# The down product of experts with 65 to 128 tokens: one slice in plain fp32, three with split operands

## The chip, the core and the metric

The kernel runs on one core of a Trainium2 chip. The metric is the device time of one execution, in microseconds (us). It is written in Bass and Tile: every engine (PE is the matrix engine, DVE the vector engine, ACT the scalar engine, POOL the GpSimd engine, SP the engine that issues most DMAs) has its own stream of instructions, and semaphores order them.

## The reference, cut to what matters

Two layers of a diffusion backbone over 1024 latent and 256 context tokens, model width 1024. Each layer ends in a mixture of 32 experts, of which every token takes two. In layer 1 1280 tokens go through it, in layer 2 1024. For the tokens `xb` of expert `e`:

```
return (jax.nn.silu(xb @ wg[e]) * (xb @ wu[e])) @ wd[e]
```

`wg` and `wu` are 1024 x 512, `wd` is 512 x 1024, all fp32: 6.3 MB for each expert. The row is then scaled by its gate and added to the token.

## The kernel before, in words

The function `moe` holds the whole of a layer's experts. They are taken in an order by size that the router writes into a table on the chip (behind the first FIX = 2), so how many tokens each step of the unrolled loop has is known only at run time: `n` is that number in blocks of 64, and `tc.If` picks one of the written variants. `n` = 1 runs `half` (64 tokens), `n` = 2 (65 to 128 tokens, the case that the change touches) runs `full`, and `n` over 2 runs `large`, which lies in the code between the test of `n` (L2345) and the other two variants (L2349).

Weights come through a ring of 14 buffers of 1 MB (the names er, es, raw, ox), six units for an expert: units 0 to 3 hold two slices each of gate and up, units 4 and 5 two slices each of `wd`. SP issues their loads in `e_loads` (L2046, L2048), four units ahead of the activation and two behind the evacuation, each when the buffer that it fills is free. So the ring runs some two experts ahead.

A product in plain fp32 is one `matmul`. A product "with split operands" is `mm3` (L173): each operand is a high part, which ACT makes by rounding to fp32r (`split`, L170), and a low part, which DVE makes as the difference (L171); then three fp32r products are added up (high x high L175, low x high L176, high x low L177). `full` (L2132) forms gate and up so: eight slices `k`, each of two halves `o`, 48 matmuls. The split weights lie in four pairs of buffers WS[0] to WS[3] (wh, wl). Slices 0 to 2 are split ahead by `prep` (L2097) together with the tokens (xh, xl); slice `k` + 3 is split while slice `k` is multiplied, and slices 6 and 7 are multiplied half by half.

Behind `full` each engine goes on in this order:

- DVE copies two columns of places (L2364); ACT forms the silu of both halves (L2163) and DVE multiplies (L2164) into sg.
- PE transposes the next expert's tokens xg (L2082) and sg (L2170) in turns; ACT copies the transposed sg to g (L2171), and ACT and DVE copy the next expert's tokens to xT (L2087, L2088).
- `down` (L2177) multiplies g by `wd` in plain fp32: four slices for each of two halves, 8 matmuls of 128 x 512 (L2181) into py[0] and py[1]. ACT and DVE have no work in it.
- If the next expert has `n` > 1, `prep` splits its slices 0 to 2 and its tokens (L2393): on ACT wh, xh, wh, xh, wh, on DVE wl, xl, wl, xl, wl.
- `evac` copies py[0] on ACT (L2186) and py[1] on DVE (L2187) to my. SP issues the next loads, POOL scatters my to memory (L2195).
- Then the next expert's test of `n` follows, and in its `full` ACT and DVE begin with the split of slice 3.

So ACT and DVE meet `prep`, then the evacuation, then slice 3, strictly in this order.

Of the kernel before, what the change touches and what calls it, by code (L numbers as in the profile page):

```python
# [10 lines left out]
F32R = mybir.dt.float32r  # L11
# [34 lines left out]

FIN = {'G': 'AAAPPPPP', 'C': 'PPPDPDDD', 'E': 'AAAAAAAA', 'N': 'SPSPSPSS'}
P1 = {'C': 'DPDPPPPDPP', 'E': 'AADAADDDAA', 'N': 'SSDSPSPDSS', 'W': 'DPDDDDDP', 'W2': 'DPPDDDDP', 'H': 'DDPDDDPDDP', 'V': 'AADDADDAADDAAADDADAA', 'U': 'AADAD'}
# [11 lines left out]
class Plan:  # L60
# [7 lines left out]
    def add(self, eng, length, f, deps=(), rank=(0.0, ""), at=0.0, take=None, give=(), after=None):  # L68

        e = [eng] if isinstance(eng, str) else list(eng)
        n = [length] if isinstance(eng, str) else list(length)
        fs = [f] if isinstance(eng, str) else list(f)
        k = len(self.ops)
        self.ops.append((list(zip(e, n, fs)), sorted({d for d in deps if d is not None}), rank, at, take, after))
        for g in give:
            self.givers.setdefault(g, []).append(k)
        return k
# [65 lines left out]
class Kernel:  # L145
# [555 lines left out]
    def plan1(self, order, sp, below, raws, Wh, Wl, PS, load, where, pb):  # L701
# [126 lines left out]
        def block_ops(n):  # L828
# [66 lines left out]
            def close(j):  # L895
                ps = PS[b, j]
                ip, ic = where((b - CT // 2 if last else b) * 256)
                if j == 0:
                    if P1["U"][n] == "D":
                        v.tensor_copy(self.U[:, :, ip:ip + 256], ps)  # L900
                    else:
                        act.activation(self.U[:, :, ip:ip + 256], ps, AF.Copy)
                    return
                v.tensor_tensor(self.A[:, j - 1, ic:ic + 256], ps[:, 1, :], sgs[j], op=OP.mult)
            sgs = {}

            def sigm(j):
                sgs[j] = below.tile([128, 256], F32, name="sg", bufs=2)
                act.activation(sgs[j], PS[b, j][:, 0, :], AF.Sigmoid)
# [23 lines left out]
            for j in range(3):  # L933
# [3 lines left out]
                else:  # L937
                    x = add(ACT, 0.26, lambda j=j: sigm(j), [ends[j]] + ([SG[m - 3]] if m > 3 else []))
                    SG[m] = CL[m] = add(DVE, 0.34, lambda j=j: close(j), [x, ma])

        SG, W2L = {}, []
        tile_ops(0)
# [1108 lines left out]
    def moe(self):  # L2051
        tc, nc, l = self.tc, self.nc, self.l
        nt = self.nt
        T = nt * 128
        with ExitStack() as ctx:
            sp = ctx.enter_context(self.pool(f"ms{l}", bufs=1))
# [5 lines left out]
            py = [pp.tile([128, 512], F32, name=f"mpy{o}", bufs=1) for o in range(2)]  # L2062
            scat = []
            self.ring += [wp.tile([128, 2048], F32, name=f"es{i}") for i in range(NU - NU0)]
            WS = [(wp.tile([128, 1024], F32R, name=f"wh{i}"), wp.tile([128, 1024], F32R, name=f"wl{i}")) for i in range(NS)]
            G = [sp.tile([128, 4, 128], F32, name=f"g{i}") for i in range(2)]
            SG = [sp.tile([128, 256], F32, name=f"sg{i}") for i in range(2)]
            iv = sp.tile([128, 3], I32, name="iv")
            XT = [sp.tile([128, KD, 128], F32, name=f"xT{i}") for i in range(2)]
# [20 lines left out]
            def xt(x, n):  # L2090
                xt_copy(xt_pe(x), n)
# [33 lines left out]
            def prod(ps, i, k, ns=NS, os=range(2)):  # L2125
                h, lo = [w.rearrange("p (s n) -> p s n", s=2) for w in WS[k % ns]]
                for o in os:
                    c = slice(o * 256, o * 256 + 256)
                    self.mm3(ps[o], XS[i][0][:, k, :], XS[i][1][:, k, :], h[:, :, c], lo[:, :, c],
                             k == 0, k == KD - 1)  # L2130

            def full(ps, e, x=None):  # L2132

                for k in range(KD - 2):
                    if k + AHEAD < KD:
                        ws(e, k + AHEAD)
                    prod(ps, 0, k)
                for o in range(2):
                    for k in range(KD - 2, KD):
                        prod(ps, 0, k, NS, (o,))  # L2140
                    if x is not None and o == 0:
                        xt(x, e)

            def double(ps, p2, e, m):

# [15 lines left out]
            def act(ps, o):  # L2161
                sg = SG[o]
                nc.scalar.activation(sg, ps[o][:, 0:256], AF.Silu)  # L2163
# [13 lines left out]
            def down(g, e, hf, os=range(2)):  # L2177
                for k, o in [(k, o) for k in range(4) for o in os] if hf else [(k, o) for o in os for k in range(4)]:
                        c = slice(o * 512, o * 512 + 512)
                        z = k // 2 * 64  # L2180
                        nc.tensor.matmul(py[o][64 * o:64 * o + 64, :] if hf else py[o],  # L2181
                                         g[:, k % 2, z:z + 64] if hf else g[:, k, :],
                                         self.unit(e, 4 + k // 2)[:, k % 2, c], start=(k == 0), stop=(k == 3))
# [151 lines left out]
            for e in range(NE):  # L2335
                n = N.pop(e)
                nxt = e + 1 if e + 1 < NE else None
                if e + 3 < NE:
                    load_n(e + 3)
                if e + 2 < NE:  # L2340
                    gather(xg[e % 2], first(e + 2, 0, "a"))
                ps, p2, y, y2, g, g2 = GU[e % 2], GU[1 - e % 2], Y[e % 2], Y[1 - e % 2], G[e % 2], G[1 - e % 2]
                if e < NE // 2:

                    with tc.If(n > 2, preferred_fallthrough_block=True) as c:  # L2345
                        large(e, n, ps, p2, y2, g2)
                        nc.tensor.addr_align(256, offset=0, max_nops=0)
                    with c.Else():
                        with tc.If(n > 1, preferred_fallthrough_block=True) as c2:  # L2349
                            full(ps, e)  # L2350
                        with c2.Else():
                            half(ps, e)
                else:
                    with tc.If(n < 2) as c:
                        half(ps, e)
                    with c.Else():
                        with tc.If(n > 2) as c2:
                            large(e, n, ps, p2, y2, g2)
                        with c2.Else():
                            full(ps, e)  # L2360
                self.e_loads(e * 6 + 4 + NU)
                pl = sp.tile([128, 2], I32, name="pl", bufs=4)
                for o, z in enumerate((self.idx_v, self.idx_w)):
                    nc.vector.tensor_copy(pl[:, o:o + 1], z[:, 0, at(e)])  # L2364
                if e + 3 < NE:
                    over(e + 3)
                s0, s1 = act(ps, 0), act(ps, 1)
                if nxt:
                    x = xt_pe(xg[nxt % 2], (0,))
                ht(ps, s0, g, 0)  # L2370
                if nxt:
                    x += xt_pe(xg[nxt % 2], (1,))
                ht(ps, s1, g, 1)
                if nxt:
                    xt_copy(x, nxt)
                if e < NE // 2:
                    with tc.If(n > 2, preferred_fallthrough_block=True) as c:
                        large_down(e, n, p2, y2, g, g2, pl)
                    with c.Else():
                        with tc.If(n > 1, preferred_fallthrough_block=True) as c2:  # L2380
                            down(g, e, False)
                        with c2.Else():
                            down(g, e, True)
                else:
                    with tc.If(n < 2) as c:
                        down(g, e, True)
                    with c.Else():
                        with tc.If(n > 2) as c2:
                            large_down(e, n, p2, y2, g, g2, pl)
                        with c2.Else():  # L2390
                            down(g, e, False)
                if nxt:
                    with tc.If(N[nxt] > 1):  # L2393
                        prep(nxt)
                evac(y)
                self.e_loads(e * 6 + 6 + NU)
                scatter(y, [pl[:, o:o + 1] for o in range(2)])
                if e >= NE - 3:
                    self.marks.append(nc.gpsimd.memset(self.spacer, 0.0))
                if e == 2:  # L2400
                    self.route_gates()

    def final(self):
# [3 lines left out]
        with ExitStack() as ctx:  # L2407
# [14 lines left out]
            def tile_ops(i):  # L2422
# [7 lines left out]
                if i > 4:  # L2430
                    XL[i] = add(DMA, 1.45, lambda: self.comb_xload(t), [Y.get(3)])
                if FIN["G"][i] == "A":
                    x = add(ACT, 1.04, lambda: self.comb0a(i, t), [y])
# [115 lines left out]
```

## Time and profile before

| what | us |
|---|---|
| median of 3 runs | 3205.91 |
| lowest and highest run | 3199.2, 3206.66 |
| the profiled execution, its own time | 3205.89 |
| its span, first to last instruction | 3204.1 |
| PE busy | 2653.9 |
| DVE busy | 1507.2 |
| ACT busy | 1187.7 |
| POOL busy | 1064.8 |

The profiled execution took what the median took (0.02 us apart), and 1.8 us of it lie outside its span. Its mean granted TensorE clock is 0.916 of full speed. Busy shares are averages over very different stages: layer 1's experts run from about 876 to 1640 us of the span, layer 2's from about 2390 to 3138.

### The profile page before, as it was taken

The page shows a single profiled execution, that of the slowest core. Times are in us where ns is not written, and L with a number is a line of the kernel's source. Part 1 is how long each engine was busy: PE and PEld are TensorE (multiplying, and loading weights), DVE is VectorE, ACT ScalarE, POOL GpSimd, SP SyncE. Part 2 cuts the span into 40 slices and gives each one's busy share as a digit, 9 for nine tenths or more (in the row PEclk, how much of TensorE's full clock was granted, in tenths as well). Part 3 has the DMA queues.
Part 4 walks back from the last instruction along what each step waited for, and adds up shares of the span by engine and source line. Part 5 has one row for each costly group of instructions (what it writes and reads, how often), then busy time and mean ns, then how long its engine had stood idle before and what let it go on. Part 6 is the DMA issues. An engine that isn't in the chain of part 4 may idle for free. (4 is left out here: it accounts for less than half of the span.)

```text
span 3204.1 us, 43663 instructions
## 1 busy us (share of the span) xinstructions
PE 2653.9 (83%) x13122; PEld 1670.8 (52%) x13122; DVE 1507.2 (47%) x2981; ACT 1187.7 (37%) x2260; POOL 1064.8 (33%) x919
## 2 busy tenths in 40 slices
PE   6988899998489888987748989999848888887873
PEld 3766556576356445543317765566634455632321
DVE  3355556477644345521149555556852335511115
ACT  3223766632043334511135337665202335511112
POOL 1023999223311121111236349941331111112214
PEclk8988999999699999999978999999969999999987
DMA  7542000042665558899985530002274457799995
GB/s 268 216 139 81 1 1 1 1 157 79 236 245 189 198 181 307 311 351 361 349 315 186 185 136 1 1 1 99 86 260 167 158 196 267 294 363 369 354 357 238
DMA packets 280646, 617.02 MB, mean 193 GB/s; under 512 B 63376, under 2 KB 77072, under 8 KB 271504
## 3 DMA queue, kind: packets, MB, share of 16 engines
q1 hardware_dynamic: 253872, 566.43, 49.0%
q0 software_dynamic: 24544, 37.91, 3.4%
q8 instruction: 281, 4.60, 0.6%
q10 hardware_dynamic: 1536, 4.69, 0.4%
q14 instruction: 413, 3.38, 0.3%
HBM read 577.09 MB, written 73.81 MB: 203 GB/s over the span
## 5 line engine op out<-in xcount | busy, mean ns | idle before, releaser
L2195 POOL DMA_INDIRECT y_d<-my,pl x150 | 166.1, 1107 | 451.2 <-ACT wh L170 194.5
L1330 DVE TENSOR_REDUCE mx<-S 128x1 f32<-128x1024 f32 (+1 forms) x272 | 215.3, 799 | 210.7 <-PE S L1325 210.4
L2181 PE MATMUL mpy<-er,g 128*64 128x512 f32 (+1 forms) x656 | 239.7, 665 | 6.9 <-issue 6.7
L2194 POOL MEMSET spacer<- 128x1 f32 x152 | 17.5, 115 | 665.9 <-DMA y_d<-my,pl 520.5
L175 PE MATMUL gu<-wh,xh 128*128 128x512 f32 x432 | 183.2, 424 | 47.1 <-issue 12.6
L2082 PE MATMUL mtp<-ident,xg 128*128 128x128 f32 x600 | 107.2, 314 | 138.9 <-issue 85.6
L2163 ACT ACTIVATE sg<-gu 128x256 f32<-128x256 f32 x152 | 50.3, 383 | 461.3 <-PE gu L2115 313.9
L1342 ACT ACTIVATE P<-S,nb 128x256 f32<-128x256 f32 (+1 forms) x272 | 208.3, 772 | 33.5 <-DVE nb L1334 32.2
L1356 ACT ACTIVATE PT<-pt 128x512 f32<-128x512 f32 (+1 forms) x321 | 169.1, 531 | 138.2 <-PE pt L1347 129.5
L1347 PE MATMUL pt<-ident,P 128*128 128x128 f32 x1312 | 207.2, 283 | 11.3 <-ACT P L1342 11.1
L2164 DVE TENSOR_TENSOR sg<-gu,sg 128x256 f32<-128x256 f32 x152 | 57.7, 420 | 334.9 <-ACT sg L2163 308.1
L1391 PE MATMUL po<-PT,V 128*64 128x256 f32 x1312 | 215.0, 408 | 0.1
L181 POOL TENSOR_TENSOR rs_out<-ln_ve,mhalf 128x1 f32<-128x1 f32 x64 | 58.7, 917 | 451.0 <-DVE ln_ve L200 292.6
L1347 PEld LDWEIGHTS pt<-ident,P 128*128 128x128 f32 x1312 | 145.2, 141 | 85.5 <-ACT P L1342 42.2
L176 PE MATMUL gu<-wl,xh 128*128 128x512 f32 x432 | 179.5, 416 | 8.9 <-DVE wl L171 8.8
L177 PE MATMUL gu<-wh,xl 128*128 128x512 f32 x432 | 177.4, 411 | 0.0
L2082 PEld LDWEIGHTS mtp<-ident,xg 128*128 128x128 f32 x600 | 82.6, 162 | 178.2 <-issue 167.1
L2115 PE MATMUL gu<-er,xT 128*64 128x512 f32 x704 | 162.2, 607 | 12.3 <-DMA er<-in_w_e_gate 4.8
L1324 PE MATMUL S<-KH,Q 128*128 128x512 f32 (+1 forms) x400 | 168.3, 422 | 1.6 <-ACT P L1342 1.6
L2187 DVE COPY my<-mpy 128x512 f32<-128x512 f32 x75 | 51.7, 690 | 233.9 <-PE mpy L2181 217.6
L171 DVE TENSOR_TENSOR wl<-er,wh 128x1024 fp32r<-128x1024 f32 x106 | 128.1, 1222 | 70.6 <-ACT wh L170 62.7
L1222 POOL TENSOR_TENSOR Y<-Y 128x1310 f32<-128x1310 f32 (+1 forms) x60 | 150.6, 2510 | 5.0
(407 smaller groups left out, 6350.4 us busy)
## 6 DMA issues: line engine op xcount, KB each, us to landing
er<-in_w_e_down SPq DMA_DIRECT2D x66, 1024.0 KB
er<-in_w_e_gate SPq DMA_DIRECT2D x130, 512.0 KB
er<-in_w_e_up SPq DMA_DIRECT2D x130, 512.0 KB
raw<-in_w_mod SPq DMA_DIRECT2D x40, 1024.0 KB
es<-in_w_e_gate SPq DMA_DIRECT2D x68, 512.0 KB
es<-in_w_e_up SPq DMA_DIRECT2D x68, 512.0 KB
es<-in_w_e_down SPq DMA_DIRECT2D x32, 1024.0 KB
raw<-in_w_e_gate SPq DMA_DIRECT2D x40, 512.0 KB
```

Of the source, the lines that this page charges most:

```text
L175: t.matmul(ps, lh, rh, start=start, stop=False)
L176: t.matmul(ps, lh, rl, start=False, stop=False)
L177: t.matmul(ps, ll, rh, start=False, stop=stop)
L1324: tens.matmul(x[:, c:c + w], q, self.KH[:, g, o:o + w], start=True, stop=False)
L1330: v.tensor_reduce(S[st, "mx"][:, ci:ci + 1], S[st, ci][:, 0:cs[ci][1]], axis=AX.X, op=OP.max)
L1342: act.activation(P[st][:, c:c + w], S[st, ci][:, :w], AF.Exp, bias=S[st, "nb"], accum_out=SU[pi][:, i, h, ci:ci + 1])
L1347: tens.transpose(tp[:, j, :], P[st][:, (g_ * 4 + j) * 128:(g_ * 4 + j + 1) * 128], self.ident)
L1356: act.activation(d, TP[st, g_][:, :m, :], AF.Copy)
L1391: tens.matmul(PO[key][o * 64:o * 64 + 64, :], self.V[:, k0(pi) + j, hp // 2, :], PT[pi, 2 * hp + o][:, j, :], start=(j == 0), stop=(j == n ...
L2082: nc.tensor.transpose(tp[:, j, :], x[:, k * 128:(k + 1) * 128], self.ident)
L2181: nc.tensor.matmul(py[o][64 * o:64 * o + 64, :] if hf else py[o], g[:, k % 2, z:z + 64] if hf else g[:, k, :], self.unit(e, 4 + k // 2)[:, ...
L2195: s = nc.gpsimd.indirect_dma_start(out=self.y_d[0:2 * T, :].rearrange("t (h d) -> (t h) d", h=2), out_offset=bass.IndirectOffsetOnAxis(ap= ...
```

## The change

A new pair of buffers GS holds the high and low parts of three slices of g. For `n` = 2, `full` also splits the down weights' slice 1 ahead of its last 12 matmuls (`wd(e, 1)` into WS[1]), and `down3` takes the place of `down`: slice 0 of both halves stays a plain fp32 product, then g's slices 1 to 3 are split, and slices 1 to 3 are products with split operands, slices 2 and 3 of the weights being split there into WS[2] and WS[3]. The other variants (`half`, `large`) keep their `down`.

```
+            GS = [sp.tile([128, 3, 128], F32R, name=f"gs{i}") for i in range(2)]
...
-            def full(ps, e, x=None):
+            def full(ps, e, x=None, dn=False):
+
 
                 for k in range(KD - 2):
                     if k + AHEAD < KD:
                         ws(e, k + AHEAD)
                     prod(ps, 0, k)
+                if dn:
+                    wd(e, 1)
                 for o in range(2):
                     for k in range(KD - 2, KD):
                         prod(ps, 0, k, NS, (o,))
                     if x is not None and o == 0:
                         xt(x, e)
+
+            def wd(e, k):
+
+                self.split(*WS[k], self.unit(e, 4 + k // 2)[:, k % 2])
+
+            def down3(g, e):
+
+                gh, gl = GS
+                for o in range(2):
+                    nc.tensor.matmul(py[o], g[:, 0, :], self.unit(e, 4)[:, 0, o * 512:o * 512 + 512], start=True, stop=False)
+                self.split(gh, gl, g[:, 1:4, :])
+                for k in range(1, 4):
+                    if k > 1:
+                        wd(e, k)
+                    h, lo = WS[k]
+                    for o in range(2):
+                        c = slice(o * 512, o * 512 + 512)
+                        self.mm3(py[o], gh[:, k - 1, :], gl[:, k - 1, :], h[:, c], lo[:, c], False, k == 3)
...
-                            full(ps, e)
+                            full(ps, e, dn=True)
...
-                            down(g, e, False)
+                            down3(g, e)
```

The last two edits are made in both forms of the loop's body (experts 0 to 15 and 16 to 31).

## Rows read from the trace of the kernel before

**Rows 1.** Windows: busy us (and instructions) of PE, PEld, DVE, ACT, POOL; clock, DMA share, GB/s.
```profile
1178.00:1386.00 208.00, 188.84 (x684) 124.64 (x684) 110.86 (x146) 100.05 (x138) 29.14 (x43) 0.96 0.82 299
1390.00:1600.00 210.00, 164.72 (x748) 68.26 (x744) 31.49 (x87) 31.17 (x75) 35.60 (x56) 0.91 1.00 362
```
**Rows 2.** Waits of PE, 1178 to 1386: us in total, times, longest us.
```profile
PE gu L175 <- DVE my L2187: 6.7, 7, 1.0
PE gu L175 <- ACT wh L170: 5.1, 4, 1.9
PE gu L2170 <- DVE sg L2164: 4.5, 9, 0.5
...
PE gu L176 <- DVE wl L171: 2.8, 4, 0.8
```
**Rows 3.** The same view, 2655 to 2816.
```profile
PE gu L2170 <- DVE sg L2164: 3.5, 7, 0.5
```
**Rows 4.** Timeline of PE: the one early expert of 65 to 128 tokens in layer 1.
```profile
894.76 0.77 PE L175 MATMUL gu<-wh,xh 128*128 128x512 f32 x1 [3.82 <-DVE wl L171]
```
**Rows 5.** Timeline of PE, one expert: start us, us, instruction, count, idle before it.
```profile
1258.25 0.39 PE L175 MATMUL gu<-wh,xh 128*128 128x512 f32 x1
...
1258.48 0.39 PE L176 MATMUL gu<-wl,xh 128*128 128x512 f32 x1
...
1261.02 7.11 PE L2181 MATMUL mpy<-raw,g 128*128 128x512 f32 x16
...
1269.07 0.47 PE L175 MATMUL gu<-wh,xh 128*128 128x512 f32 x1 [0.95 <-DVE my L2187]
```
**Rows 6.** Timeline of the weight loads inside another plain down product.
```profile
1196.12 0.19 PEld L2181 LDWEIGHTS mpy<-es,g 128*128 128x128 f32 x1 [0.24 <-issue]
...
1196.55 0.19 PEld L2181 LDWEIGHTS mpy<-es,g 128*128 128x128 f32 x1 [0.24 <-issue]
```
**Rows 7.** Timeline of ACT and DVE beside the down product of rows 5.
```profile
1261.18 0.38 ACT L2171 ACTIVATE g<-gu 128x256 f32<-128x256 f32 x1 [0.27 <-PE gu L2170]
...
1261.46 0.59 ACT L2087 ACTIVATE xT<-mtp 128x512 f32<-128x512 f32 x1
1262.52 1.06 ACT L170 ACTIVATE wh<-er 128x1024 fp32r<-128x1024 f32 x1 [0.46 <-ACTq L2377]
...
1263.61 1.22 DVE L171 TENSOR_TENSOR wl<-er,wh 128x1024 fp32r<-128x1024 f32 x1 [1.95 <-ACT wh L170]
...
1264.75 0.68 DVE L171 TENSOR_TENSOR xl<-xT,xh 128x512 fp32r<-128x512 f32 x1
...
1267.35 0.60 ACT L2186 ACTIVATE my<-mpy 128x512 f32<-128x512 f32 x1 [0.84 <-ACT wh L170]
...
1268.22 0.68 DVE L2187 COPY my<-mpy 128x512 f32<-128x512 f32 x1
```
**Rows 8.** Timeline: slice 3's split in the expert from 1247.63, which went undisturbed.
```profile
1246.80 1.06 ACT L170 ACTIVATE wh<-es 128x1024 fp32r<-128x1024 f32 x1 [0.38 <-ACT my L2186]
...
1248.34 1.23 DVE L171 TENSOR_TENSOR wl<-es,wh 128x1024 fp32r<-128x1024 f32 x1 [0.67 <-DMA er<-in_w_e_down]
```
**Rows 9.** Timeline: slice 3's split in experts where ACT, and once DVE, came late.
```profile
1273.33 2.95 ACT L170 ACTIVATE wh<-er 128x1024 fp32r<-128x1024 f32 x3 [5.38 <-issue]
...
1368.93 1.22 DVE L171 TENSOR_TENSOR wl<-es,wh 128x1024 fp32r<-128x1024 f32 x1 [6.10 <-issue]
```
**Rows 10.** Waits of ACT, 1178 to 1386.
```profile
ACT wh L170 <- issue: 16.5, 3, 5.7
```
**Rows 11.** Windows: the 8 us around the late split of 1273, columns as in rows 1.
```profile
1272.00:1280.00 8.00, 6.25 (x20) 4.42 (x19) 5.53 (x5) 4.96 (x5) 0.00 (x0) 0.79 0.64 241
```
**Rows 12.** Timeline of ACT in layer 2: one of the two late splits there.
```profile
2772.56 3.90 ACT L170 ACTIVATE wh<-es 128x1024 fp32r<-128x1024 f32 x4 [5.49 <-issue]
```
**Rows 13.** Timeline: behind an expert of 129 to 192 tokens, PE and DVE.
```profile
1134.48 0.40 PE L175 MATMUL gu<-wh,xh 128*128 128x512 f32 x1
...
1134.63 0.69 DVE L2187 COPY my<-mpy 128x512 f32<-128x512 f32 x1
```

More of the change, by code (lines that the diff above doesn't have):

```diff
@@ L2359, in moe @@
                         with c2.Else():
-                            full(ps, e)
+                            full(ps, e, dn=True)
                 self.e_loads(e * 6 + 4 + NU)
@@ L2390, in moe @@
                         with c2.Else():
-                            down(g, e, False)
+                            down3(g, e)
                 if nxt:
```

## The prediction

> **What bounds the kernel now.** I read the page first: PE is the busiest engine, with 2653.9 of 3204.1 us. That is an average, so next I read the windows of the two stages that matter [rows 1]. In layer 1's stage of 65 to 128 tokens (1178 to 1386 us) PE is busy 188.84 of 208 us and the DMA engines 0.82 of the time; in the stage of up to 64 tokens behind it the DMA share is 1.00 at 362 GB/s. So the changed stage is bound by PE and what it waits for, and the next one by the loading of weights. As the weight ring is full at the border, what the changed stage gains or loses moves the end of the kernel one to one.
>
> Which experts are touched: PE waits once in each of them for DVE's multiplication (L2170 on sg), 9 times in layer 1's stage [rows 2] and 7 in layer 2's [rows 3]; one more begins at 894.76 [rows 4]. That makes 17 experts. In 14 places one of them is followed by another (8 and 6), at two by one of 64 tokens, and at one by a larger one.
>
> Then I read one such expert in the timeline, PE first [rows 5], then ACT and DVE [rows 7]. Times below are from the start of its down product, 1261.02. Before: ACT's copy of g is done at 0.54 and of xT at 1.03, ACT begins `prep` at 1.50, DVE sits idle for 1.95 until its first split at 2.59 and is then full until its copy of py[1] ends at 7.88. PE ends the down product at 6.86 and begins the next expert at 8.05; the profile puts that gap down to DVE's copy, or to its next instruction. Slice 3's split, the first thing behind the evacuation, is undisturbed 0.71 to 1.94 us behind PE's start [rows 8], while PE wants it after 18 products, so DVE has 2.5 us to spare. In 5 transitions it is disturbed: ACT stands for 5.4 to 5.7 us between its evacuation and that split and waits for nothing that the profile shows [rows 9, 10, 12], and in a sixth DVE does so for 6.10 [rows 9]. Then PE waits for the high and again for the low part, and its granted clock falls to 0.79 in the 8 us around [rows 11].
>
> **The change, part by part.**
>
> *PE.* A plain product is two records 0.43 apart [rows 6], so 0.86, and eight are 6.86. fp32r products start 0.23 to 0.24 apart [rows 5], I take 0.2345. The new down product is 2 x 0.86 + 18 x 0.2345 = 5.94, 0.92 less; 17 times that is 15.6 us, the gain if nothing else moved.
>
> *ACT and DVE.* Added in the down product: the split of 128 x 384 of g and two splits of 128 x 1024. ACT: 0.50 (between 0.38 for 256 and 0.59 for 512 columns) and twice 1.0. DVE: 0.55 (from 0.68 for 512) and two steps of 1.14, the step from one split to the next [rows 7]. That is 2.5 and 2.8 us, in front of `prep`, on engines that go in order. Laid out: high part of g 1.1 to 1.6, its low part 1.7 to 2.25; slice 2 on ACT 1.55 to 2.6, on DVE 2.7 to 3.9; slice 3 on ACT to 3.55, on DVE 3.85 to 5.05. PE: the plain slice to 1.72, which covers the split of g; slice 1 to 3.13; slice 2's second product waits for DVE until 3.95, the slice ends at 5.1; slice 3 then finds its split just ready and ends at 6.5. So the down product gains 0.33 and not 0.92: DVE takes the rest back.
>
> *What is queued behind.* `prep` on ACT now begins at 4.0 (the gap of 0.46 kept), on DVE at 5.15; its five splits take the 4.61 that they took [rows 7], so DVE's copy of py[1] ends at 10.45 instead of 7.88, and ACT's of py[0], whose 0.84 of waiting mostly goes, near 9.0 instead of 6.93. PE begins the next expert 0.33 earlier, at 7.72: what it needs first (splits of slice 0 and of the tokens, at 7.05) is there, and slices 1 and 2 come in time (8.2 and 9.95 against 9.4 and 10.8). I keep the gap of 1.19 between PE's last product and its start; bounds are 1.0 (if it follows PE's own queue) and 3.9 (if it follows DVE's copy, 10.45 + 0.17). I take the first kind, since behind a larger expert the next one's products run before DVE's copy has begun [rows 13]. Slice 3's low part, 0.9 behind DVE's copy, is there at 12.65; PE wants it at 7.72 + 19 x 0.2345 = 12.18. So an undisturbed transition gains 0.33 and loses some 0.45: I take +0.1, between -0.6 and +1.2.
>
> *Disturbed transitions.* The 5.4 us follow ACT's evacuation, which is 2.0 later: the split is 2.0 later, and nothing of PE's covers it, since PE waits there already. 5 x 2.0 = 10.0; for the one where DVE stands, 2.0. Below: 0, if the stall ends at a fixed time; above: 3.0 with a longer fall of the clock.
> I read these stalls as the loading of code at the jump over `large`: same place, same length, about every third expert. [...]
>
> *The rest.* The split of the down weights' slice 1 needs WS[1], free 12 products (2.81 us) ahead of the end of `full`; ACT needs 1.04 and DVE 1.22 behind it, done at 2.4: hidden; were the cover gone, silu (behind it on ACT) and the multiplication (behind it on DVE) would be up to 1.2 later. No DMA is added; units 4 and 5 come free up to 2 us earlier, which a DMA share of 0.82 does not need. POOL's scatter goes 2 us later, which nobody waits for within an expert. The two borders to 64 tokens gain 0.33 each; the one to a larger expert I count as 0, as ACT and DVE have no slice 3 to hurry for there.
>
> Sum: 8 x 0.1 + 10.0 + 2.0 - 0.7 = +12.1. The profiled execution took 3205.89, as the median did: 3218.
>
> **The rivals.**
>
> *Hidden after all (ends faster).* If ACT and DVE get through the added splits faster than laid out, by the 0.5 us that slice 2 and slice 3 of the next expert lack, each of the 17 experts gains up to 0.92 and disturbed transitions lose less than a microsecond: between -15.6 and -8, 3195 in the middle. For it: 1.95 idle on DVE and 2.5 to spare at slice 3 against 2.8 added. Against: the spare time is spent to the last half microsecond, and the disturbed ones have none. It decides at the end of DVE's copy: under 9.9, PE sets the pace.
>
> *It cancels.* The disturbed stalls end at a time of their own and not a fixed time behind ACT; then only the undisturbed sum and half of PE's gain remain, -5 to +5: 3206.
>
> *The stalls move.* Three of fourteen stalled: a stall costs now some 3.7 (about 2.0 of waiting [rows 2], and 8 us at a clock of 0.79, 1.7 [rows 11]) and would then cost 5.7, so 3 x 5.7 against 5 x 3.7: -1, the time the same. Eight: 45.6 against 18.5, +27: 3233. For it: the stalls return every third expert. Against a forecast from it: I can't tell which.
>
> *The buffers bind.* `prep` writes slices 1 and 2 into WS[1] and WS[2], which the down product now reads. If it waits for the end of the product and not of the slice, ACT's `prep` stands from 5.6 to 6.6, slices 2 and 3 come 1 to 2 us late in all 14: +14 to +28 on top, 3239.
>
> **How the numbers follow.** About 0.3% is what a measurement of this kernel can tell from no change, 9.6 us, so 3196.3 to 3215.5 is "the same". Forecast, DVE-paced with later stalls (+4 to +22): 0.42, a quarter of it below the bound. Hidden: 0.17. Cancels or fewer stalls: 0.24, of it 0.03 faster. More stalls or bound buffers: 0.17. That gives faster 0.20, the same 0.33, slower 0.47. The range leaves out a tenth at each side: 3193 to 3243; the forecast's own is 3210 to 3228.
>
> **What would show it.** The down product of these experts 6.3 to 6.7 long instead of 6.86, with PE waiting for DVE's wl in slice 2; DVE's copy of py[1] 10.2 to 10.7 behind its start; PE waiting for wl in slice 3 by some tenths in undisturbed experts; the late splits still 5.4 behind ACT's evacuation and PE's wait there 2 us longer. The forecast is wrong if DVE's copy ends under 9.9, if the number of stalls changes by two or more, or if PE's gap at the next expert's start grows by over 0.5.

## The result and the profile after

The changed kernel takes 3278.04 us (median of 4 runs, 3274.42 to 3282.09), the kernel before 3202.55 beside it (4 runs, 3193.07 to 3206.66): a ratio of 1.024, 95% interval 1.0212 to 1.0269. So it is slower by some 75 us, where 12 were forecast and a range that ended at 3243. The profiled execution took 3282.09 with a span of 3279.6, 75.5 more than the span before; its mean granted clock is 0.902 against 0.916.

Windows of the changed kernel, columns as in [rows 1]: the changed stage of layer 1, that of layer 2, and two stretches at the start of one expert.
```profile
1175.00:1414.00 239.00, 191.31 (x740) 141.36 (x742) 148.39 (x184) 128.78 (x174) 39.50 (x45) 0.88 0.72 262
2689.00:2884.00 195.00, 150.84 (x576) 111.16 (x578) 115.50 (x146) 99.41 (x134) 33.53 (x39) 0.87 0.70 255
1282.50:1287.50 5.00, 4.94 (x12) 3.91 (x13) 0.87 (x1) 1.06 (x1) 1.14 (x2) 0.51 0.80 286
1287.50:1296.00 8.50, 8.50 (x38) 6.81 (x37) 5.39 (x7) 4.25 (x4) 0.10 (x1) 1.00 0.12 46
```
In layer 1's stage PE was busy for 188.84 of 208 us [rows 1] and is now for 191.31 of 239. The work has hardly grown, the idle time has gone from 19 to 48 us. From its first product to the first one of the stage behind it, that stage takes 208.03 us before and 238.65 after (+30.6), layer 2's 162.05 and 193.67 (+31.6). Two more pieces lie outside. From the end of the last expert's last product to the first product of the next stage (L284) it is 157.6 us before and 167.7 after at the end of layer 1 (+10.1); from the end of layer 2's last expert to the end of the span it is 66.2 and 76.0 (+9.8). The rest, some -7, is spread over the stretches between.

The longest waits of PE in layer 1's stage, changed kernel: us in total, times, longest us.
```profile
PE gu L175 <- DVE wl L171: 21.9, 4, 5.6
PE gu L175 <- issue: 15.9, 3, 6.0
PE gu L175 <- DVE cola L2238: 6.8, 2, 4.4
PE gu L2192 <- DVE sg L2186: 4.5, 9, 0.5
```
Of the kernel before, [rows 2] leave out one row of the same view:
```profile
PE gu L175 <- DVE cola L2216: 3.2, 1, 3.2
```
The wait for sg is the same 4.5 in both. At L175 PE now waits 44.6 us in 9 places, all of them the start of an expert, where it waited 15.0 us in 12 places, 11.8 of it at these nine starts. The profile names two releasers for this one gap, or none. The timeline of one expert shows what lies in it (start us, us, instruction, count, idle before it).
```profile
1270.55 1.95 PE L2156 MATMUL mpy<-raw,g 128*128 128x512 f32 x4
1271.47 0.53 ACT L170 ACTIVATE gs<-g 128x384 fp32r<-128x384 f32 x1
1272.09 0.56 DVE L171 TENSOR_TENSOR gs<-g,gs 128x384 fp32r<-128x384 f32 x1 [0.91 <-ACT gs L170]
1272.97 2.36 DVE L171 TENSOR_TENSOR wl<-raw,wh 128x1024 fp32r<-128x1024 f32 x2 [0.32 <-ACT wh L170]
1273.74 0.39 PE L175 MATMUL mpy<-wh,gs 128*128 128x512 f32 x1
1274.26 0.50 PE L176 MATMUL mpy<-wl,gs 128*128 128x512 f32 x1
1275.25 1.22 DVE L171 TENSOR_TENSOR wl<-er,wh 128x1024 fp32r<-128x1024 f32 x1
1276.70 0.39 PE L177 MATMUL mpy<-wh,gs 128*128 128x512 f32 x1
1277.67 0.59 ACT L2208 ACTIVATE my<-mpy 128x512 f32<-128x512 f32 x1
1279.86 0.69 DVE L2209 COPY my<-mpy 128x512 f32<-128x512 f32 x1
1280.46 0.15 DVE L2238 COPY cola<-idx_g 128x1 int32 x1
1282.56 0.77 PE L175 MATMUL gu<-wh,xh 128*128 128x512 f32 x1 [5.47 <-DVE wl L171]
```
Read from the down product's start at 1270.55: slice 3's low part is there at 4.78 (1272.97 + 2.36), the last product ends at 6.54, DVE's copy at 10.0. The next expert begins only at 12.01, 5.47 us behind PE's last product and 2.0 behind DVE's copy. Slice 0's low part, which the first products read, was ready at 5.9 (1275.25 + 1.22) and the copy of cola, the other releaser named, at 10.1; the experiments below show that the start waits for none of the later splits either.

What does lie in that gap is a transfer of code ("instruction" in the view of the DMA queues). The changed kernel from 1279.4 to 1280.9 (packets, MB, share):
```profile
q8 instruction: 1, 0.02, 4.5%
```
One packet of 0.02 MB of instructions lands here, and none on this queue from 1275.2 to 1279.4 or from 1280.9 to 1283; PE begins 1.8 us later. In the expert of [rows 5] the same packet comes between 1266.2 and 1267.4, while the plain down product still runs. (One more packet starts 3.1 to 3.7 us behind each of the first eight products of layer 1's stage, in both kernels alike; it is not the one that moved.)

At layer 1's end the changed kernel's timeline has the last scatter, the first load of the next stage on SP's queue and the first work on what a later load brings.
```profile
1670.61 0.98 POOL L2217 DMA_INDIRECT y_d<-my,pl  x1 [0.19 <-issue]
1673.60 0.34 SPq L214 DMA_DIRECT2D g<-mod_d  x1
1677.50 1.88 SPq L424 DMA_DIRECT2D yy<-y_d  x3
1689.87 1.15 ACT L435 ACTIVATE yy<-yy,gates 128x1024 f32<-128x1024 f32 x1 [0.95 <-DMA yy<-y_d]
```
The load of g is issued 3.0 us behind the scatter, and it is 19.3 us from the scatter to ACT. In the kernel before that load is issued 18.7 us ahead of the scatter, and ACT follows the scatter by 9.6.
```profile
1623.75 0.35 SPq L214 DMA_DIRECT2D g<-mod_d  x1
1642.45 0.98 POOL L2195 DMA_INDIRECT y_d<-my,pl  x1 [0.19 <-issue]
1647.16 1.56 SPq L424 DMA_DIRECT2D yy<-y_d  x3
1652.08 1.15 ACT L435 ACTIVATE yy<-yy,gates 128x1024 f32<-128x1024 f32 x1 [4.23 <-DMA yy<-y_d]
```

### The profile page after: what moved, and what is told of

It reads as the page before. It is cut to its first block, busy times and chain, and to the rows that moved or that the text cites. A ratio compares the mean times of both kernels' runs of the same rounds, so it can differ in the third digit from the quotient of the medians.

```text
span 3279.6 us, 44262 instructions
## 1 busy us (share of the span) xinstructions
PE 2653.2 (81%) x13224; PEld 1704.5 (52%) x13224; DVE 1576.7 (48%) x3049; ACT 1244.6 (38%) x2328; POOL 1084.7 (33%) x919
## 5 line engine op out<-in xcount | busy, mean ns | idle before, releaser
L2217 POOL DMA_INDIRECT y_d<-my,pl x150 | 184.6, 1230 | 525.0 <-ACT my L2208 168.4
L175 PE MATMUL gu<-wh,xh 128*128 128x512 f32 x432 | 191.9, 444 | 103.7 <-issue 56.0
L1347 PE MATMUL pt<-ident,P 128*128 128x128 f32 x1312 | 207.3, 283 | 10.9 <-ACT P L1342 10.5
L171 DVE TENSOR_TENSOR wl<-er,wh 128x1024 fp32r<-128x1024 f32 x129 | 156.5, 1223 | 100.7 <-ACT wh L170 92.1
L177 PE MATMUL gu<-wh,xl 128*128 128x512 f32 x432 | 184.5, 427 | 0.0
L170 ACT ACTIVATE wh<-er 128x1024 fp32r<-128x1024 f32 x129 | 135.2, 1059 | 121.5 <-PE gu L177 87.7
L2203 PE MATMUL mpy<-er,g 128*64 128x512 f32 (+1 forms) x528 | 176.3, 650 | 1.4 <-issue 1.2
L175 PEld LDWEIGHTS gu<-wh,xh 128*128 128x128 f32 x432 | 91.0, 211 | 140.5 <-issue 115.5
```

Source lines behind the costliest of these rows:

```text
L175: t.matmul(ps, lh, rh, start=start, stop=False)
L177: t.matmul(ps, ll, rh, start=False, stop=stop)
L1347: tens.transpose(tp[:, j, :], P[st][:, (g_ * 4 + j) * 128:(g_ * 4 + j + 1) * 128], self.ident)
L2217: s = nc.gpsimd.indirect_dma_start(out=self.y_d[0:2 * T, :].rearrange("t (h d) -> (t h) d", h=2), out_offset=bass.IndirectOffsetOnAxis(ap= ...
```

## The experiments

Two questions stood: what makes the gap at the next expert's start, and what makes the borders longer. For the gap there were three theories: **the added splits** on ACT and DVE hold it; **the length** of the product's instruction stream does (supposing that PE takes only so many instructions in ahead); **the late wait** does (supposing that PE's sequencer does not pass a product whose wait is not met, so that the jump over `large` and the loading of the code behind it start only when the last wait inside the down product is met). In all that follows R is the time of that last wait and GU the start of the next expert's gate and up, both counted from the start of the down product. Of the kernel before R is 0.54 (ACT's copy of g, [rows 7]) and GU 8.05; of the changed one R is 4.78 and GU 10.9 to 12.5 (layer 1's stage).

**The splits without their products.** From the changed kernel: `down3` keeps its ACT and DVE work, PE does the plain eight products.

```diff
 def down3(g, e):
     gh, gl = GS
-    for o in range(2):
-        nc.tensor.matmul(py[o], g[:, 0, :], ...
     self.split(gh, gl, g[:, 1:4, :])
-    for k in range(1, 4):
...
+    for k in range(2, 4):
+        wd(e, k)
+    down(g, e, False)
```


> The change with its splits on ScalarE and VectorE as they are (slice 1 during gate and up, gate and slices 2 and 3 in the down block), but TensorE's down product plain, as before: 8 plain products whose operands lie ready when the block begins. Theory W (wait): TensorE's sequencer does not go past a product whose wait is not yet met, so the jump over the code of the larger experts starts only when the last wait of the down product is met (4.8 us after its start in the changed kernel), and the next expert's first product comes about 7 us after that. Here no product waits: gap after the last down product 0.9 to 1.1 us as before, gate and up 11.5 us, time 3190 to 3215. Theory C (chain): the later splits on ScalarE and VectorE hold TensorE: gap 4 to 6 us, time about 3270. Theory L (length): the 20 products in place of 8 make the jump late: as W here, 3190 to 3215.

Measured: 3211.9, ratio 1.0039 (1.0016 to 1.0061). The timeline of one expert:
```profile
1237.15 1.95 PE L2197 MATMUL mpy<-er,g 128*128 128x512 f32 x4
1245.16 0.47 PE L175 MATMUL gu<-wh,xh 128*128 128x512 f32 x1 [0.90 <-ACT my L2202]
1246.44 0.68 DVE L2203 COPY my<-mpy 128x512 f32<-128x512 f32 x1
```
GU is 8.01, as before (over both stages 8.0 to 9.0 in either kernel), though DVE's copy ends at 9.97, behind it. The two stages take 204.0 and 162.5 us, against 208.0 and 162.1. So 2.5 us more on ACT and 2.8 on DVE, in front of everything that the prediction counted as late, cost nothing in the stages. The 15 us that remain against its own runs of the kernel before (3197.2) lie outside the stages, at the two layers' ends (10.0 and 9.8 us longer), and are the second question's.

**The products without their splits.** The changed kernel's PE products on operands that are there long before: GS is split once from other data, and `wd` and g's split are left out.

> The change with TensorE's down product as it is (2 plain and 18 split products), but without the splits of the gate and of slices 1 to 3: the products read operands that were split earlier from other data, so no product waits when the block begins. What is left out: those splits, so the down product of 65 to 128 tokens is of other numbers. Theory W: the next expert's first product comes 7.4 to 8.1 us after the start of the down product (gap 0.9 to 1.6 us in place of 4.4 to 6.0), gate and up 11.5 us, time 3185 to 3210. Theory L: gap 4 to 6 us stays, time 3255 to 3285. Theory C: gap about 0.9, time 3185 to 3200.

Measured: 3256.49, ratio 1.0182 (1.0147 to 1.0216). Layer 2's tokens go to other experts here, so layer 1's stage alone compares. Its timeline:
```profile
1232.82 1.96 PE L2154 MATMUL mpy<-er,g 128*128 128x512 f32 x4
1238.59 0.40 PE L177 MATMUL mpy<-wh,gs 128*128 128x512 f32 x1
1241.94 0.77 PE L175 MATMUL gu<-wh,xh 128*128 128x512 f32 x1 [2.95 <-DVE cola L2233]
```
The product is 6.17 us long, GU 9.12. None of the three theories had it so: W expected 7.4 to 8.1, L a gap of 4 to 6 where it is 2.95. So the length costs about 1.1 us with no late wait in it: it is a part, but length alone does not make 12.

**Fewer products.** The same with one split slice in place of three: 12 products instead of 20, so 36 weight loads and products in PE's stream in place of 44 (a plain product is two of each).

> As e2, but one slice of the four by split products and three plain: 12 products (6 plain, 6 split) in place of 20. No product waits on a split. Left out: the split that belongs to it. e2 left 1.1 us open (first product of the next expert 9.12 us after the start of the down product, 8.03 in the kernel before). Theory L2 (the sequencer runs ahead by a limited number of instructions; in e2 at its release time some 34 of the 44 loads and products of the block were left): here the block holds 36, so next to nothing is left, and the next expert's first product comes 7.9 to 8.3 us after the start, as with the plain block of 32. Theory F (the split form itself makes it late): about 9.1. Time between the kernel before and e2.

Measured once: 3261.6 us (layer 2 goes another way again); GU in layer 1's stage 7.96 to 8.54, mostly 8.2. With 36 nearly nothing is lost, with 44 one us. That would fit a limit on how far the sequencer runs ahead of PE. GU of 9.12 less the 7.5 us of the kernel before (8.05 - 0.54) puts the jump's begin at 1.6, when some 10 of the 44 have started and 34 are left. This limit is an estimate from these kernels and was not tested further.

**A late wait alone.** The kernel before, its plain products kept; only the last of the eight reads a copy of g that POOL makes in a chain of four (long) or two (short) steps.

```diff
+    down(g, e, False, (0,))
+    z = g[:, 1:4, :]
+    for i in range(4):
+        nc.gpsimd.tensor_copy(GX[i % 2], z)
+        z = GX[i % 2]
+    for k in range(4):
+        nc.tensor.matmul(py[1], z[:, 2, :] if k == 3 else g[:, k, :], ...
```


> The kernel before with one late wait: of the 8 plain down products the last reads a copy of the gate that GpSimd makes by a chain of 4 copies of 128x384, started when the gate is there. Should the chain end R us after the start of the down product, and R be under 6.2 us, TensorE itself loses nothing by it. Theory W: the next expert's first product comes at R + 6.1 to 7.7 us; with R about 4.5 the gap is 3.5 to 5 us, gate and up grows to 13 us by the clock, time 3245 to 3290. Theories L and C: gap 0.9 to 1.1, time 3195 to 3212.

> As e3 with 2 copies in place of 4, R about half. Theory W: the gap follows R: with R about 2.3 the next expert's first product at 8.4 to 10 us after the start of the down product, gap 1.3 to 2.9 us, time 3210 to 3245, between the kernel before and e3. Theories L and C: gap 0.9 to 1.1, time 3195 to 3212.

Measured: long 3254.12, ratio 1.0168 (1.0128 to 1.0208); short 3229.71, ratio 1.009 (1.0054 to 1.0126). Timeline of the long one:
```profile
1235.53 1.96 PE L2193 MATMUL mpy<-er,g 128*128 128x512 f32 x4
1236.66 1.65 POOL L2150 COPY gx<-gx 128x384 f32<-128x384 f32 x3
1241.61 1.02 PE L2153 MATMUL mpy<-ox,gx 128*128 128x512 f32 x2
1245.66 0.60 PE L175 MATMUL gu<-wh,xh 128*128 128x512 f32 x1 [3.03 <-issue]
```
The short one:
```profile
1236.72 1.96 PE L2193 MATMUL mpy<-er,g 128*128 128x512 f32 x4
1237.86 0.51 POOL L2150 COPY gx<-gx 128x384 f32<-128x384 f32 x1
1245.67 0.48 PE L175 MATMUL gu<-wh,xh 128*128 128x512 f32 x1 [1.84 <-DVE cola L2228]
```
POOL's chain ends 2.78 and 1.65 behind the start, some 3 us and more before the product that reads it is due, so PE's products lose nothing. Yet GU is 10.12 to 10.41 and 8.92 to 9.4. In both it is R + 7.3 to 7.8, and in the kernel before 8.05 - 0.54 = 7.5 (R + 7.5 to 8.5 over its transitions): the time of the last wait sets the start, though the products lose nothing. The instruction packet goes with it. In the experts shown it comes from 5.15 to 6.3 behind the product's start in the kernel before, 7.4 to 8.5 in the long one, 9.1 to 10.2 in the changed one. Not all of the 57 and 33 us that these two kernels lose is the wait's: their tiles gx lie where the changed kernel has GS, and layer 1's end is as long as there (167.2 and 171.7 us), which is the second question's.

**The jump taken away.** If the late wait costs by holding back a far jump, it should cost nothing where the next expert's code is near. Experts 8 to 31 lose the variant for more than 128 tokens, which none of them runs here; once from the kernel before, once from the changed one.

```diff
-                if e < NE // 2:
+                if 8 <= e < NE // 2:
+                    with tc.If(n > 1, preferred_fallthrough_block=True) as c:
+                        full(ps, e)
+                    with c.Else():
+                        half(ps, e)
...
```


> The kernel before without the code for more than 128 tokens at experts 8 to 31 (none of them has more in this run, so the result is the same; what is left out is code that does not run here). So behind an expert of 65 to 128 tokens the next one's code follows without a far jump. Theory W with the far jump as what takes the 7.4 us: the gap of 0.9 to 1.9 us behind the down product goes to 0 at these experts (13 times), and the 3.9 to 4.3 us between the experts of up to 64 tokens in the second layer too: 3160 to 3190. If the 7.4 us are not the jump's: gap and time as before, 3195 to 3210.

> The changed kernel with the same code left out (more than 128 tokens at experts 8 to 31). Its late waits are all there, the far jump is not. Theory W: the gap of 4.4 to 6.0 us goes to 0 to 0.5, gate and up back to 11.5 us, so time within 12 us of e6, 3165 to 3195. Theory C (ScalarE's and VectorE's later splits hold TensorE): the gap stays 4 us or more, time 45 to 75 us over e6.

Measured: from the kernel before 3109.21, ratio 0.9729 (0.9704 to 0.9753); from the changed one 3135.33, ratio 0.9802 (0.9778 to 0.9827). The first, its window and its timeline:
```profile
1168.00:1350.00 182.00, 177.53 (x684) 120.01 (x684) 115.30 (x150) 100.46 (x139) 39.24 (x47) 1.00 0.93 343
```
```profile
1221.66 1.97 PE L2181 MATMUL mpy<-er,g 128*128 128x512 f32 x4
1228.22 0.80 PE L175 MATMUL gu<-wh,xh 128*128 128x512 f32 x1
```
The second, its timeline:
```profile
1223.32 1.97 PE L2156 MATMUL mpy<-er,g 128*128 128x512 f32 x4
1227.06 0.50 PE L176 MATMUL mpy<-wl,gs 128*128 128x512 f32 x1
1229.73 0.40 PE L175 MATMUL gu<-wh,xh 128*128 128x512 f32 x1
```
GU is 6.56 and 6.41: no gap, in the changed kernel as little as in the other, though its waits for the splits are all still there. That settles the late wait as the cause **together with** the far jump. Code packets agree; the counts of queue q8 in the stage of nine experts, kernel before, then the one without the code:
```profile
q8 instruction: 27, 0.44, 0.9%
```
```profile
q8 instruction: 9, 0.15, 0.3%
```
That is three packets for each expert with the jumps, one without.

Two things were missed. The first kernel came out 50 us below its expected range: not only the gaps went, but also the late splits of [rows 9] (ACT's 5.4 to 5.7 and DVE's 6.10, none is left), the clock in the stage is 1.00, and experts of up to 64 tokens take 12.5 us each at 385 GB/s. And the second, itself 30 below its range, is 26 above the first, where at most 12 were expected. By the traces 12.5 of it lie at the border of the layers, 9.0 behind layer 2's last expert, and 4.0 at one far jump that is left in layer 2, behind expert 6 (GU 12.29 against 8.30).

**Waits closer together.** In the kernel before both transposes of the next tokens go ahead of those of sg.

```diff
-                ht(ps, s0, g, 0)
                 if nxt:
                     x += xt_pe(xg[nxt % 2], (1,))
+                ht(ps, s0, g, 0)
                 ht(ps, s1, g, 1)
```


> The kernel before with one line moved: the second group of transposes of the next expert's rows goes ahead of the first transposes of the hidden rows, where TensorE waited 0.5 us for them. Theory W: the last wait of the plain down product is the second half of the gate, copied 0.54 us after the product's start; it comes some 0.35 us sooner, and so does the jump: 0.3 to 0.5 us per expert of 65 or more tokens, 3188 to 3198 in all, ratio 0.996 to 0.999. If the second hidden rows come too late for it, no difference.

Measured: 3195.96, ratio 0.9992 (0.9978 to 1.0006), GU 7.7 to 8.3. No difference in time is shown. R came 0.3 to 0.4 sooner and the mean of GU went from 8.22 to 8.04 over 14 transitions, less than the scatter among them: this run neither confirms the theory nor speaks against it.

**The borders: the place of GS.** The kernel before, with the two GS tiles beside its own and nothing else of the change; they are written once.

```diff
+            GS = [sp.tile([128, 3, 128], F32R, name=f"gs{i}") for i in range(2)]
...
+            self.split(*GS, XT[0][:, 1:4, :])
```


> The kernel before plus the change's two gate tiles (3072 B of each partition in the pool of the expert stage), written once per layer and read by nothing that counts. Behind the experts every kernel that has such tiles (the changed one, e1 to e5, e7) took 169 to 174 us from its last expert product to the next layer's first product of line 284, those without (before, e6, f1) 156 to 162. Theory M (place): the tiles push the index tiles of the last scatters under the buffers of the next stage, whose loads then start only after the scatters, 10 to 12 us per layer: 3215 to 3222, the expert stage itself as before. Theory N (the 12 us have another cause, late scatters of the changed down product): as before, 3192 to 3202.

Then the changed kernel with GS in the pool of the weights, as it is and without the code for larger experts:

```diff
-            GS = [sp.tile([128, 3, 128], F32R, name=f"gs{i}") for i in range(2)]
+            GS = [wp.tile([128, 3, 128], F32R, name=f"gs{i}") for i in range(2)]
```


> The changed kernel with its two gate tiles in the pool of the expert weights, which lies behind that of the expert stage, so that the next stage's buffers meet the same tiles as in the kernel before. Theory M: the next stage's loads start early again, 18 to 24 us less than the changed kernel, 3252 to 3262; the gaps of 4.4 to 6.0 us stay. Theory N: 3270 to 3284.

> e7 (the changed kernel without the code for more than 128 tokens at experts 8 to 31) with the gate tiles in the weight pool. In e6 and e7 one expert of 65 to 128 tokens took 20.23 and 20.21 us, so the change was worth nothing there; what e7 had over e6 should be the tiles' place (some 20 us) and one far jump behind the down product in the second layer (4.6 us). Theory M: 3110 to 3118, the change itself 0 to 8 us over e6 (3109). Theory N: as e7, 3135.

Measured: the kernel before with GS 3211.46, ratio 1.0037 (1.0022 to 1.0052), so +13; the changed one with GS elsewhere 3264.01, ratio 1.0209 (1.0178 to 1.0241), 66 us over its own runs of the kernel before where the change is 75 over its own, so some 10 less (14 by the bare medians); that one without the code 3117.86, ratio 0.9752 (0.9725 to 0.978), 17 less than with the tiles in their old place. Timeline of the kernel before with GS, at the border:
```profile
1639.20 0.98 POOL L2196 DMA_INDIRECT y_d<-my,pl  x1 [0.19 <-issue]
1642.18 0.34 SPq L214 DMA_DIRECT2D g<-mod_d  x1
1645.96 1.77 SPq L424 DMA_DIRECT2D yy<-y_d  x3
1658.46 1.15 ACT L435 ACTIVATE yy<-yy,gates 128x1024 f32<-128x1024 f32 x1 [0.95 <-DMA yy<-y_d]
```
The 19.3 of the changed kernel are here with two tiles alone, and 167.3 from the last expert's last product to L284. The changed kernel with GS elsewhere has 8.3 and 156.7, and its load of g is issued ahead of the scatter again, by more than 6.6 us (SP's queue issues none from 1667 on, with the scatter at 1673.64); that of yy comes 3.5 behind the scatter. The addresses in the built programs say why: 3072 bytes of GS move the places `pl`, which the last scatters read, from 78656 .. 78760 to 81728 .. 81832, and the next stage's buffer g2 (the profile's `g` of L214) lies at 81632 .. 85728. So its load, the first in SP's queue, waits for the last scatters (issued 2.98 us behind the last one, where it is 18.7 ahead in the kernel before), and the loads behind it wait with it (that of yy comes 6.8 behind the scatter, there 4.7). At layer 2's end the same shift puts `pl` (80960 .. 81064) under another buffer, cxt (80992 .. 85088). The size was expected higher (3215 to 3222), and so was the release in the changed kernel (18 to 24); without the code it came into the range (3110 to 3118).

**Code that cannot run.** Experts are sorted by size behind the first two, so no more than 2T / 129 of the others can have over 128 tokens, whatever the routing (19 in layer 1, 15 in layer 2). The variants for more are left out of the kernel before from there on.

```diff
-                        with tc.If(n > 2) as c2:
-                            large(e, n, ps, p2, y2, g2)
-                        with c2.Else():
+                        if e < FIX + 2 * T // 129:
+                            with tc.If(n > 2) as c2:
+                                large(e, n, ps, p2, y2, g2)
+                            with c2.Else():
+                                full(ps, e)
+                        else:
                             full(ps, e)
```


> The kernel before without the code for more than 128 tokens at those experts that can never have them: the experts behind the first two run in the order of their counts, so of 2T places at most 2T/129 can exceed 128, 19 of the first layer and 15 of the second; the code goes from expert 21 on in the first layer and from 17 on in the second. Nothing of the result is left out. There an expert of up to 64 tokens jumps over that code between gate and up and the transposes, where TensorE waits 2 to 4 us each time. Theory W (the far jump): those waits shrink to below 1 us until the weight loads bind, 15 to 45 us less than before, 3150 to 3182. If the loads bind already: 3185 to 3200.

Measured: 3160.67, ratio 0.9891 (0.9863 to 0.992), inside the theory's range. This beats both kernels, by 1.1% and more. PE's longest waits from 2900 to 3100, first this kernel, then the kernel before:
```profile
PE gu L2115 <- DMA er<-in_w_e_up: 16.6, 16, 1.9
PE gu L2115 <- DMA es<-in_w_e_up: 5.7, 9, 1.2
```
```profile
PE mtp L2082 <- issue: 26.2, 9, 3.9
```
The 26.2 us without a releaser are gone, and what PE waits for is now the weights.

## Why the prediction was wrong, step by step

- **PE's product** was laid out as 6.5 long and is 6.54, with the wait for DVE in slice 2 (1273.74 to 1274.26). Right.
- **What is queued behind on ACT and DVE**: DVE's copy was to end at 10.45 and ends at 10.0; ACT's copy was put near 9.0 and ends at 7.7. Too late by 0.45 and 1.3, the order right. The wait for DVE in slice 3 of the next expert, on which the +0.1 of an undisturbed transition rests, does not show at all: PE's waits in the two stages hold no row for it. That PE does not follow DVE's copy was right too: with the plain product it starts ahead of that copy's end.
- **"I keep the gap of 1.19 between PE's last product and its start; bounds are 1.0 (...) and 3.9".** This is the step that failed. In layer 1's stage the gap is now 4.4 to 6.0, in layer 2's once 7.6: above both bounds. (The second bound should have read 4.1: 10.45 + 0.17 - 6.5.) I took it for a cost behind the product's end, or for a wait on DVE. It is the end of a chain that starts at the last wait *inside* the product: R, then some 7.5 us for the jump and its code. The old product hid most of it (7.5 of code against 6.3 of products behind the wait), so only a sixth of its size was to be seen in [rows 5]. The change put R from 0.54 to 4.78, with 1.8 us of products behind it. [Rows 13], which I chose as the nearest, show a transition from one larger expert to the next; queue q8 carries no packet of code from 1124.1 to 1140 there, so it has no such chain and could say nothing of this case. Nearer rows of the same trace do: at the passage from the larger experts to this stage PE stands for 3.2 us, and the gap of 3.82 in [rows 4] lies behind a short product, one of up to 64 tokens (below), where R is 0.41 and GU 7.47, so R + 7.1. The code loading was read on ACT alone; for PE no rival had it.
```profile
887.29 3.65 PE L2181 MATMUL mpy<-er,g 128*64 128x512 f32 x16
```
- **Its price**: over the 15 transitions with the jump the mean of GU goes from 8.25 to 11.95, +3.7, or 55.6 us; the border behind layer 1's stage, which has no gap in either kernel, gains 0.7. That is 55 of the two stages' 62 us. Behind the longer idle time PE's granted clock is 0.50 to 0.60 in the first 5 us of the next expert (eight starts of layer 1's stage; in the kernel before 1.00 from 1269.07 to 1274.07), and gate and up take 13.3 to 14.0 instead of 11.48. Over both stages gate and up take 7 us more, the rest of the 62, and not more than that since the kernel before had waits for late splits there (one expert's gate and up took 17.2). The two layers' ends add 20 and the other stretches give back 7, which makes the 75.
- **"Disturbed transitions"**, 5 x 2.0 + 2.0: nothing of it. With the splits alone the stages get 4.0 us shorter and 0.4 longer, and in the changed kernel's view of ACT's waits the row of [rows 10] is gone from layer 1. Late splits have not gone: layer 2 keeps two on ACT (10.5 us), and DVE now stands so twice in each layer (3.3 to 4.6 us), where it did once in all. But PE's waits hold no row for any of them.
- **"The rest"** looked at queues and semaphores and not at where the new tiles lie: 10 us at the end of each layer by the traces, +13 in the whole time, shown with the tiles alone.
- **The rivals.** *Hidden after all* is what ACT and DVE did, but its gain never came: without the jump the old product and the new one give the same, GU 6.56 and 6.41, 20.23 and 20.21 us from one expert to the next, and whole kernels at 0.9729 and, with GS in the other pool, 0.9752, intervals that overlap. *The buffers bind* did not occur. *The stalls move* had the right cause, code loading at the jump, on the wrong engine; that added code moves the stalls to other experts was a supposition, and what the traces show of it stands above: ACT has none in layer 1, where it had three, and two in layer 2 as before, DVE two in each. The falsifier that the gap grows by over 0.5 is the one that struck.

Left open: what fills the 4.6 us between the last wait and the start of the packet, and the 1.7 behind its landing; why the changed kernel's GU spreads over R + 6.1 to 7.7, and once 9.4, where the kernels with one late wait keep to 7.3 to 7.8.

## What to carry to other kernels

Where unrolled loops branch on run-time sizes, look for the last semaphore wait of an engine ahead of each far jump, and count from there, not from the end of the work: a shorter product whose last wait is later can lose more than it saves (here 6.54 us in place of 7.11, last wait at 4.78 in place of 0.54, and the next expert starts 3.7 later behind the product's start). Take the row of a transition only from one that jumps as far and has as much work behind its last wait. Code that cannot run is worth leaving out (1.1% here), and tiles are worth adding in a pool whose growth moves nothing that the next stage loads early (13 us here).

## What the runs showed of the hardware

- In the two kernels with one late wait, PE's first product of the next expert, behind a far jump, came 7.3 to 7.8 us after that wait was met. In the expert shown of the long one it was 4.6 until a packet of 0.016 MB of code began to move (27 such packets are 0.44 MB), 1.1 for it, 1.6 behind.
- Moving one wait of one product by 1.1 us (1.65 to 2.78) moved the next expert by 1.2 (the mean of GU from 9.05 to 10.24 in layer 1's stage), though that product came some 3 us and more behind its wait.
- Code that never ran cost 2.7% of this kernel (3109.21 us without it, 3196.78 with it): the gaps of PE and the late splits on ACT and DVE (5.4 to 6.1 us) were gone without it.
- Behind a gap of 5.47 us without a product (changed kernel, to 1282.56) the granted clock was 0.51 for the next 5 us.
- 3072 bytes of tiles, with no work on them, cost 13 us: they moved a tile that is read late onto the buffer that the next stage loads first.
